# Gated products of two feed-forward sublayers as seven block products (Strassen) in a two-layer hybrid backbone

## The chip, the cores and the metric

The kernel runs on one core of a Trainium2 chip. The metric is the device time of one execution in microseconds (us). TensorE (PE) multiplies, VectorE (DVE) and ScalarE (ACT) do elementwise work, GpSimd (POOL) does little, and SyncE (SP) issues the DMAs. The kernel before took 2584.07 us, the median of three runs (2581.18 to 2584.51).

## The reference

Two streams of 256 tokens each, the latent tokens x and the context tokens ctx, of width D = 1024, go through two layers. A layer is a feed-forward sublayer, a mixer and another feed-forward sublayer; each is modulated by vectors that come from a conditioning vector (adaLN) and closed by a layer norm. In the last layer the context leaves after the first feed-forward sublayer has fed it to the mixer.

```python
def swiglu(u, w1, w3, w2):
    return (jax.nn.silu(u @ w1) * (u @ w3)) @ w2

def ffn_sublayer(h, mod, w1, w3, w2, g, b):
    u = h * (1 + mod[1]) + mod[0]
    return layer_norm(ALPHA * h + 0.5 * mod[2] * swiglu(u, w1, w3, w2), g, b)

# per layer l, with the same weights for both streams
x = ffn_sublayer(x, ada_x[0], ffn_w1[l, 0], ffn_w3[l, 0], ffn_w2[l, 0], ...)
xc = ffn_sublayer(xc, ada_c[0], ffn_w1[l, 0], ffn_w3[l, 0], ffn_w2[l, 0], ...)
# mixer of both streams, then the sublayer with index 1 (in the last layer for x alone)
```

Here w1 and w3 are 1024 x 2816 and w2 is 2816 x 1024, all in fp32. 2816 columns are FT = 22 tiles of 128.

## The kernel before, in words

Everything is kept feature-major: a tile holds 128 features in its partitions and tokens along its free axis, columns 0 to 255 (`XR`) for x and 256 to 511 (`CR`) for ctx. Three feed-forward sublayers work on 512 tokens, `ffn(0,0)`, `ffn(0,1)` and `ffn(1,0)` (layer, index); the last one, `ffn(1,1)`, on the 256 of x.

Each fp32 product is done as three products of rounded parts. `wchunk` (L186) loads a 128 x 1024 weight chunk into a buffer `raw` by an SP DMA of 512 KB, ACT writes its rounded part `whi` (L196), and DVE the remainder `wlo` (L197). The moving operand has the same two parts, made by `split_into` (L200 to L202). `mm3` (L208) then issues, for each of the 8 pieces of 128 input features, whi times high, whi times low, and wlo times high (L214, L215, L216), all into one PSUM bank.

In `ffn` the function `gated` makes the 22 tiles of silu(u @ w1) * (u @ w3): per tile two weight chunks, 2 x 8 x 3 = 48 matmuls of 512 columns, a silu on ACT (L471), a multiplication on DVE (L472) and a split into `gh` (ACT) and `gl` (DVE). The tiles are consumed in three groups, 0 to 5, 6 to 13 and 14 to 21: tiles up to one past a group are made first, then the group is multiplied by its w2 chunks, 8 chunks per group, added to the residual by DVE (L418). The last group closes the sublayer with the layer norm (`closing`).

The vectors of adaLN are made in between. `ada_job` loads pieces of w_ada (512 KB each) and DVE multiplies and adds them into accumulators `acc` (L247, L249), 32 instructions of 512 columns per job with two streams, half as many with one stream. The jobs wait in a queue; each `wchunk` lets some steps of it be issued (`tick`, with the rates RA0, RA1, RA2, in hundredths of a step), in three batches: J0 = 7 jobs during `ffn(0,0)`, J1 = 4 during `ffn(0,1)`, and the other 5 during `ffn(1,0)`.

The order on each engine is set by a scheduler: it issues what is ready, in program order, and weight work is moved ahead by 140 instructions (`PRE`). Buffers come from pools with a fixed number of slots: 4 for `raw` (NR), 5 each for the high and low weight parts (NW), 34 (NS) and 14 (NA) for 128 x 512 tiles.

Of the kernel before, what the change touches and what calls it, by code (L numbers as in the profile page):

```python
# [51 lines left out]
def hybrid_kernel(tc, x, ctx, pos, cc, wada, pcol, w1, w3, w2a, w2b, wst, wv, wg, wbr, wout, dfc, dft, idn, lnrow, out):  # L52
# [76 lines left out]

    RT = cst.tile([P, 512], F32, name="RT")  # L130
    RM = cst.tile([P, 512], F32, name="RM")
    RMh = cst.tile([P, 512], F32R, name="RMh")
    RMl = cst.tile([P, 512], F32R, name="RMl")
# [3 lines left out]
    nc.gpsimd.memset(RT, 0.0)  # L137
    nc.gpsimd.memset(RM, 0.0)
# [60 lines left out]

    def split_into(h, l, src):  # L200
        first = act(h, src, AF.Copy)  # L201
        return first, V.tensor_tensor(l, src, h.bitcast(F32), op=ALU.subtract)  # L202
# [15 lines left out]
    def proj(tiles, X, nk, T, halves):  # L218

        parts = [XR, CR] if halves and T == 512 else [slice(0, T)]  # L220
        for r in parts:
            for ps, W, *x_only in tiles:
                if r == XR or not any(x_only):
                    mm3(ps[:, r], W, X, range(nk), r)

# [126 lines left out]
    def new_operand(T):  # L352
        return [pair("op", T) for _ in range(KT)]

    def modulate(src, U, dt, l, sub, s, r):
        u = own("u", 3, 256, 256)
        act(u, src, AF.Identity, scale=modcol(l, sub, 0, s, dt), bias=modcol(l, sub, 1, s, dt))
        split_into(U[dt][0][:, r], U[dt][1][:, r], u)

# [61 lines left out]
    def closing(ys, l, sub, T, get_chunk, X, ks, nxt):  # L421
# [28 lines left out]
        U = new_operand(T)  # L450
# [5 lines left out]
    def ffn(l, i, X, ys, T, nxt):  # L456
        sub = 2 * i
        G = {}

        def gated(fts, halves=False):  # L460
# [6 lines left out]
            proj(tiles, X, KT, T, halves)  # L467
            for n, ft in enumerate(fts):
                p1, p3 = tiles[2 * n][0], tiles[2 * n + 1][0]
                sg = aslot("sg", T)  # L470
                act(sg, p1[:, 0:T], AF.Silu)  # L471
                V.tensor_tensor(sg, p3[:, 0:T], sg, op=ALU.mult)  # L472
                G[ft] = pair("g", T) if T == TX else (aslot("gh", T, F32R), slot("gl", T, F32R))
                split_into(G[ft][0], G[ft][1], sg)
# [3 lines left out]
        for ft in range(2, 7):  # L478
            gated([ft])
        for gi, grp in enumerate(GROUPS):  # L480
# [15 lines left out]
            for ft in range(grp[-1] + 2, min(grp[-1] + 10, FT)):  # L496
                gated([ft])
        return U

# [14 lines left out]
    def mixer(l, X, ys, nxt):  # L514
# [16 lines left out]
        for dt in range(KT):  # L531
            nc.sync.dma_start(out=hs[dt], in_=ys[dt][:, 0:TQ])
        gs = aslot("gs")
# [484 lines left out]
NA = 14  # L1018
NR = 4
# [3 lines left out]

TAIL = 4

J0 = 7
J1 = 4

RA0 = 135
RA1 = 75  # L1030
RA2 = 75
# [114 lines left out]
```

## Time and profile before

| | |
|---|---|
| median of three runs | 2584.07 us |
| the profiled execution | 2583.85 us |
| its span, first to last instruction | 2582.0 us |
| PE busy | 2527.9 us (98%) |
| DVE busy | 1791.0 us (69%) |
| ACT busy | 963.2 us (37%) |
| DMA, share of 16 engines | 43.8% |

Busy time counts the time in which at least one instruction of an engine was running. A matmul's listed duration is longer than the distance at which matmuls follow each other, since they are pipelined; what one costs is read from the starts of a run of them. The same holds, by a smaller amount, for DVE instructions that stand back to back.

### The profile page before, as it was taken

Reading aid. Unit: us, or ns where it says so; the run is one execution under the profiler, and the core shown is the slowest. Engines: PE = TensorE matmul, PEld = TensorE weight load, DVE = VectorE, ACT = ScalarE, POOL = GpSimd, SP = SyncE. Lnnn points to the kernel's source line nnn. Section 1 sums busy time; section 2 is a strip of 40 time slices with the busy share of each in tenths; the row PEclk is TensorE's granted clock in tenths of the full one; section 3 lists DMA queues with packets and bytes.
Section 4 is the critical chain, followed back from the end, with each engine's and each line's share of the span. In section 5 each row is a group of like instructions: output and inputs, shape, how many; then the busy total and the mean of one; then the engine's idle time right before and its main releaser. Section 6 shows DMA issues by size and latency. Waiting matters only on the chain.

```text
span 2582.0 us, 36788 instructions
## 1 busy us (share of the span) xinstructions
PE 2527.9 (98%) x14354; PEld 2143.6 (83%) x14354; DVE 1791.0 (69%) x3239; ACT 963.2 (37%) x1566; POOL 49.1 (2%) x124
## 2 busy tenths in 40 slices
PE   7999999999999999999999999999999999999998
PEld 4777779788778888888777788777788889999998
DVE  4786866978868765358656458544558888987665
ACT  4222235333342334235222225222236435455543
POOL 0000000010100000000000000000000000000000
PEclk9999999999999999999999999999999999999999
DMA  8565553213223223335445425544533334556563
GB/s 272 177 206 174 179 177 99 94 57 98 70 87 106 86 75 118 102 103 160 142 147 155 127 78 160 167 149 138 156 107 112 113 114 140 167 181 189 173 195 131
DMA packets 130542, 353.88 MB, mean 137 GB/s; under 512 B 12736, under 2 KB 28352, under 8 KB 130368
## 3 DMA queue, kind: packets, MB, share of 16 engines
q1 hardware_dynamic: 130368, 351.53, 43.8%
q8 instruction: 113, 1.85, 0.3%
q14 instruction: 61, 0.50, 0.1%
HBM read 344.11 MB, written 7.34 MB: 136 GB/s over the span
## 4 chain that ended last, share of the span: by engine, by line
PE 85%; DVE 9%; DMA 2%; ACT 1%; issue 1%; POOL 1%; SPq 0%; DVEq 0%; POOLq 0%; ACTq 0%
PE ffps L214 10%; PE ffps L216 10%; PE ffps L215 10%; PE w2ps L214 4%; PE w2ps L215 4%; PE w2ps L216 4%; PE clo L214 3%; PE br L215 3%; PE clo L215 3%; PE br L214 3%; PE clo L216 3%; PE br L216 2%; PE mg L214 2%; PE mg L216 2%; PE mg L215 2%; DVE wlo L197 2%
## 5 line engine op out<-in xcount | busy, mean ns | idle before, releaser
L196 ACT ACTIVATE whi<-raw 128x1024 fp32r<-128x1024 f32 (+1 forms) x498 | 520.5, 1047 | 1196.0 <-issue 278.6
L197 DVE TENSOR_TENSOR wlo<-raw,whi 128x1024 fp32r<-128x1024 f32 (+1 forms) x498 | 599.9, 1206 | 352.1 <-ACT whi L196 347.2
L214 PE MATMUL ffps<-opH,whi 128*128 128x512 f32 (+1 forms) x1120 | 428.4, 386 | 0.6 <-ACT opH L201 0.5
L215 PE MATMUL ffps<-opL,whi 128*128 128x512 f32 (+1 forms) x1120 | 428.8, 385 | 0.1
L216 PE MATMUL ffps<-opH,wlo 128*128 128x512 f32 (+1 forms) x1120 | 428.3, 384 | 0.4 <-DVE wlo L197 0.4
L510 DVE SCALAR_TENSOR_TENSOR cy<-cz,dww,cy 128x482 f32<-128x482 f32 (+29 forms) x480 | 289.1, 602 | 16.9 <-ACT cy L598 9.9
L249 DVE SCALAR_TENSOR_TENSOR acc<-araw,sc,acc 128x512 f32<-128x512 f32 x392 | 273.7, 746 | 30.0 <-DMA araw<-in_wada_dram 29.0
L214 PEld LDWEIGHTS ffps<-opH,whi 128*128 128x128 f32 x1120 | 209.8, 188 | 49.8 <-issue 4.6
L215 PEld LDWEIGHTS ffps<-opL,whi 128*128 128x128 f32 x1120 | 210.7, 188 | 46.0 <-issue 2.3
L216 PEld LDWEIGHTS ffps<-opH,wlo 128*128 128x128 f32 x1120 | 210.8, 189 | 45.7 <-issue 1.2
L214 PE MATMUL w2ps<-gh,whi 128*128 128x512 f32 x336 | 133.8, 398 | 0.0
L216 PE MATMUL w2ps<-gh,wlo 128*128 128x512 f32 x336 | 133.2, 397 | 0.0
L215 PE MATMUL w2ps<-gl,whi 128*128 128x512 f32 x336 | 133.0, 396 | 0.0
L472 DVE TENSOR_TENSOR sg<-ffps,sg 128x512 f32<-128x512 f32 (+1 forms) x88 | 54.7, 622 | 112.5 <-PE ffps L216 112.4
L214 PE MATMUL mg<-opH,whi 128*128 128x512 f32 (+1 forms) x384 | 130.0, 339 | 0.0
L216 PE MATMUL mg<-opH,wlo 128*128 128x512 f32 (+1 forms) x384 | 129.9, 338 | 0.0
L215 PE MATMUL mg<-opL,whi 128*128 128x512 f32 (+1 forms) x384 | 129.8, 338 | 0.0
L214 PE MATMUL qk<-opH,whi 128*128 128x512 f32 (+1 forms) x296 | 102.5, 347 | 0.0
L215 PE MATMUL qk<-opL,whi 128*128 128x512 f32 (+1 forms) x296 | 101.5, 343 | 0.0
L216 PE MATMUL qk<-opH,wlo 128*128 128x512 f32 (+1 forms) x296 | 101.1, 342 | 0.0
L214 PE MATMUL ffps<-op,whi 128*128 128x256 f32 x352 | 97.1, 280 | 3.2 <-ACT op L201 3.2
L215 PE MATMUL ffps<-op,whi 128*128 128x256 f32 x352 | 97.5, 279 | 0.0
(326 smaller groups left out, 5265.1 us busy)
## 6 DMA issues: line engine op xcount, KB each, us to landing
raw<-in_w_dram SPq DMA_DIRECT2D x176, 512.0 KB, 3.7
raw<-in_wst_dram SPq DMA_DIRECT2D x144, 512.0 KB, 3.5
araw<-in_wada_dram SPq DMA_DIRECT2D x128, 512.0 KB, 4.0
raw<-in_w2b_dram SPq DMA_DIRECT2D x64, 512.0 KB, 3.6
raw<-in_wbr_dram SPq DMA_DIRECT2D x48, 512.0 KB, 3.6
raw<-in_w2a_dram SPq DMA_DIRECT2D x32, 384.0 KB, 3.3
araw<-in_wada_dram SPq DMA_DIRECT2D x32, 256.0 KB, 5.4
raw<-in_wv_dram SPq DMA_DIRECT2D x16, 512.0 KB, 3.5
```

The lines of the kernel that those rows point to most:

```text
L196: act(hi, raw, AF.Copy)
L197: V.tensor_tensor(lo, raw, hi.bitcast(F32), op=ALU.subtract)
L214: PE.matmul(ps, wh, xh, start=first and i == 0, stop=False)
L215: PE.matmul(ps, wh, xl, start=False, stop=False)
L216: PE.matmul(ps, wl, xh, start=False, stop=last and i == n - 1)
L249: V.scalar_tensor_tensor(accs[s], w, c, accs[s], op0=ALU.mult, op1=ALU.add)
L472: V.tensor_tensor(sg, p3[:, 0:T], sg, op=ALU.mult)
L510: V.scalar_tensor_tensor(dv[:, :, a:b], sv[:, :, a + o:b + o], wcols[:, j:j + 1], dv[:, :, a:b], op0=ALU.mult, op1=ALU.add)
```

## The change

In `ffn(0,1)` and `ffn(1,0)` the tiles 4 to 21, 18 in each, are no longer made by `gated`. One such tile is seen as a 2 x 2 block product: the weights [w1 first half, w1 second half; w3 first half, w3 second half], each block 128 outputs by 512 input features, times the tokens [x first half, ctx first half; x second half, ctx second half], each block 512 features by 256 tokens. The variant of Strassen's method that is used takes seven block products in place of eight. It needs sums of weight blocks for each tile (`wquads`) and sums of token blocks once per sublayer (`Blocks.sums`).

`wquads` loads the two chunks, splits w1 (`wa`) and the second half of w3 (`wd`), makes four sums of 512 columns on DVE in the raw buffers, and splits the results (`wb`, `wc`). The low part of `wb` is made without DVE: ACT writes the rounded part with its sign changed, and a DMA issued by POOL adds the raw sum into it (`accum_op=ALU.add`). `block` multiplies one block: 4 pieces x 3 = 12 matmuls of 256 columns, 84 per tile. Four products of a tile, those with `wa` first half, `wc` first half, `wb` first half and `wd`, are added one after another into the bank `q1`, which ACT copies after the first three; those with `wb` second half and `wc` second half are added into `q3`, and the one with `wa` second half goes into `q2`. The work of one tile is interleaved with the end of the tile before (`more`).

Tiles 0 to 3 of these sublayers stay eight products, now as 256-column matmuls for each stream. Four constant tiles become scratch tiles of the mixer, zeroed by POOL there. The pools grow (NA 14 to 16, NR 4 to 5), and the adaLN jobs are dealt out anew: 9, 3 and 4 in place of 7, 4 and 5.

```diff
-    RT = cst.tile([P, 512], F32, name="RT")
-    RM = cst.tile([P, 512], F32, name="RM")
-    RMh = cst.tile([P, 512], F32R, name="RMh")
-    RMl = cst.tile([P, 512], F32R, name="RMl")
-    nc.gpsimd.memset(RT, 0.0)
-    nc.gpsimd.memset(RM, 0.0)
...
+    def wquads(src1, src3):
+        H = slice(0, 512), slice(512, 1024)
+        with tc.high_priority(offset=PRE):
+            raw = []
+            for src in (src1, src3):
+                t = wp.tile([P, 1024], F32, tag="raw", bufs=NR, name=nm("raw"))
+                nc.sync.dma_start(out=t, in_=src)
+                raw.append(t)
+            r1, r3 = raw
+            def halves(name, w=1024):
+                return [wp.tile([P, 1024], F32R, tag=t, bufs=NW, name=nm(name + t))[:, :w] for t in ("hi", "lo")]
+            a = halves("wa")
+            split_into(a[0], a[1], r1)
+            d = halves("wd", 512)
+            split_into(d[0], d[1], r3[:, H[1]])
+            add = dict(op=ALU.add)
+            V.tensor_tensor(r3[:, H[1]], r3[:, H[0]], r3[:, H[1]], **add)
+            V.tensor_tensor(r3[:, H[0]], r3[:, H[0]], r1[:, H[0]], **add)
+            V.tensor_tensor(r1[:, H[0]], r3[:, H[1]], r1[:, H[0]], **add)
+            V.tensor_tensor(r1[:, H[1]], r1[:, H[0]], r1[:, H[1]], **add)
+            b = halves("wb")
+            act(b[0], r3, AF.Copy)
+            act(b[1], b[0].bitcast(F32), AF.Copy, scale=-1.0)
+            nc.gpsimd.dma_start(out=b[1].bitcast(F32), in_=r3, accum_op=ALU.add)
+            c = halves("wc")
+            split_into(c[0], c[1], r1)
+        return (a, 0), (a, 512), (d, 0), (b, 512), (c, 0), (b, 0), (c, 512)
...
+    def block(ps, W, X, first):
+        (hi, lo), c = W
+        how = dict(skip_group_check=not first)
+        for k, (xh, xl) in enumerate(X):
+            wh, wl = (w[:, c + k * P:c + (k + 1) * P] for w in (hi, lo))
+            PE.matmul(ps, wh, xh, start=first and k == 0, stop=False, **how)
+            PE.matmul(ps, wh, xl, start=False, stop=False, **how)
+            PE.matmul(ps, wl, xh, start=False, stop=k == 3, **how)
...
     def modulate(src, U, dt, l, sub, s, r):
+        if isinstance(U, Blocks):
+            u = U.u[dt][:, r]
+            act(u, src, AF.Identity, scale=modcol(l, sub, 0, s, dt), bias=modcol(l, sub, 1, s, dt))
+            split_into(U.x[s][dt][0], U.x[s][dt][1], u)
+            return
...
+    class Blocks:
+        def __init__(self):
+            self.u = [slot("u") for _ in range(KT)]
+            self.x = [[pair("op", TX) for _ in range(KT)] for _ in range(2)]
+        def sums(self):
+            self.t = []
+            for k in range(4):
+                a, b = self.u[k], self.u[k + 4]
+                p, q = aslot("tp"), aslot("tq")
+                V.tensor_tensor(p[:, XR], a[:, XR], a[:, CR], op=ALU.subtract)
+                V.tensor_tensor(p[:, CR], b[:, CR], a[:, CR], op=ALU.subtract)
+                V.scalar_tensor_tensor(q[:, XR], p[:, XR], -1.0, b[:, CR], op0=ALU.mult, op1=ALU.subtract)
+                V.scalar_tensor_tensor(q[:, CR], q[:, XR], -1.0, b[:, XR], op0=ALU.mult, op1=ALU.subtract)
+                row = []
+                for src in (p, q):
+                    h, l = slot("tH", 512, F32R), slot("tL", 512, F32R)
+                    split_into(h, l, src)
+                    row += [(h[:, XR], l[:, XR]), (h[:, CR], l[:, CR])]
+                self.t.append(row)
+            self.u = None
+        def operands(self):
+            t1, t3, t2, t4 = ([row[n] for row in self.t] for n in range(4))
+            (x, c) = self.x
+            return x[:4], x[4:], t4, t1, t2, t3, c[4:]
...
-        U = new_operand(T)
+        U = Blocks() if T == 512 and (nxt[0], nxt[1]) in BLOCKS else new_operand(T)
...
+        def store(ft, g):
+            if T == TX:
+                G[ft] = pair("g", T)
+            else:
+                low = aslot if blocks and (ft < 4 or ft % 4 == 3) else slot
+                G[ft] = (aslot("gh", T, F32R), low("gl", T, F32R))
+            split_into(G[ft][0], G[ft][1], g)
...
+            if blocks:
+                for s, r in streams(T):
+                    for ps, W in tiles:
+                        mm3(ps[:, r], W, X.x[s], range(KT), XR)
+            else:
+                proj(tiles, X, KT, T, halves)
...
+        def start_blocks(ft):
+            f = dict(ft=ft, W=wquads(w1[l, i, ft], w3[l, i, ft]))
+            f["r1"], f["r3"] = bank(mmp, "q1")[:, XR], bank(mmp, "q3")[:, XR]
+            f["c"], f["v"] = aslot("cc"), aslot("cv", 256)
+            Q[:] = X.operands()
+            block(f["r1"], f["W"][0], Q[0], True)
+            act(f["c"][:, XR], f["r1"], AF.Copy)
+            block(f["r3"], f["W"][3], Q[3], True)
+            return f
+        def middle_blocks(f):
+            block(f["r1"], f["W"][4], Q[4], False)
+            act(f["c"][:, CR], f["r1"], AF.Copy)
+            r2 = bank(atp, "q2")[:, XR]
+            block(r2, f["W"][1], Q[1], True)
+            c = f["c"][:, XR]
+            V.tensor_tensor(c, r2, c, op=ALU.add)
+            act(c, c, AF.Silu)
+        def third_blocks(f):
+            block(f["r1"], f["W"][5], Q[5], False)
+            act(f["v"], f["r1"], AF.Copy)
+        def x_blocks(f):
+            block(f["r1"], f["W"][2], Q[2], False)
+            c = f["c"][:, XR]
+            V.scalar_tensor_tensor(c, f["r1"], -1.0, c, op0=ALU.mult, op1=ALU.mult)
+            V.tensor_tensor(f["v"], f["r3"], f["v"], op=ALU.add)
+        def ctx_blocks(f):
+            block(f["r3"], f["W"][6], Q[6], False)
+            c = f["c"][:, CR]
+            V.tensor_tensor(c, f["r3"], c, op=ALU.add)
+            act(c, c, AF.Silu)
+            V.scalar_tensor_tensor(c, f["v"], -1.0, c, op0=ALU.mult, op1=ALU.mult)
+            store(f["ft"], f["c"])
+        Q = []
+        open_ = []
+        def more(fts):
+            if not blocks:
...
+            for ft in fts:
+                f = start_blocks(ft)
+                if open_:
+                    x_blocks(open_[0])
+                middle_blocks(f)
+                if open_:
+                    ctx_blocks(open_.pop())
+                third_blocks(f)
+                open_.append(f)
+            if ft == FT - 1:
+                x_blocks(open_[0])
+                ctx_blocks(open_.pop())
...
         gated([0, 1], not ready)
         run_later()
-        for ft in range(2, 7):
-            gated([ft])
+        if blocks:
+            X.sums()
+            for ft in (2, 3):
+                gated([ft])
+            more(range(4, 7))
+        else:
+            more(range(2, 7))
...
+        RT, RM, RMh, RMl = aslot("RT"), aslot("RM"), aslot("RMh", 512, F32R), aslot("RMl", 512, F32R)
+        nc.gpsimd.memset(RT, 0.0)
+        nc.gpsimd.memset(RM, 0.0)
...
-NA = 14
-NR = 4
+NA = 16
+NR = 5
+BLOCKS = ((0, 2), (1, 0))
-J0 = 7
-J1 = 4
+J0 = 9
+J1 = 3
```

First place: ACT during one gated tile in the middle of `ffn(0,1)`, before the change (names end in a buffer's number).

```order
L196 ACTIVATE whi_10868<-raw_10866 128x1024
L257 ACTIVATE adar_10702<-adaps_10693 128x128
L201 ACTIVATE gh_10689<-sg_10686 128x512
L196 ACTIVATE whi_10875<-raw_10873 128x1024
L471 ACTIVATE sg_10770<-ffps_10714 128x512
```

The same place now: wb, wc, wa and wd are the weight parts above; cv and cc receive what is copied out of the banks.

```order
L220 ACTIVATE wbhi_11274<-raw_11260 128x1024
L586 ACTIVATE cv_11152<-q_1778_11149 128x256
L221 ACTIVATE wblo_11275<-wbhi_11274 128x1024
L571 ACTIVATE cc_11285<-q_1796_11283 128x256
L229 ACTIVATE wchi_11279<-raw_11258 128x1024
L229 ACTIVATE wahi_11396<-raw_11392 128x1024
L229 ACTIVATE wdhi_11400<-raw_11394 128x512
L582 ACTIVATE cc_11285<-cc_11285 128x256
L577 ACTIVATE cc_11285<-q_1796_11283 128x256
L599 ACTIVATE cc_11151<-cc_11151 128x256
L229 ACTIVATE gh_11369<-cc_11151 128x512
```

A tile had four ACT instructions (beside adaLN's `adar`), two of them on weights; it now has eleven, five of them on weights, and the first two on `wb` have a copy out of a bank between them.

Second place: PE at the same point, before the change, where one chunk ends and the next begins.

```order
L214 MATMUL ffps_10872<-opH_9505,whi_10868 128x512
L215 MATMUL ffps_10872<-opL_9506,whi_10868 128x512
L216 MATMUL ffps_10872<-opH_9505,wlo_10869 128x512
L214 MATMUL ffps_10879<-opH_9491,whi_10875 128x512
L215 MATMUL ffps_10879<-opL_9492,whi_10875 128x512
L216 MATMUL ffps_10879<-opH_9491,wlo_10876 128x512
```

And now, where the low part of `wb` is read for the first time by a tile (`q_1815` is its bank q3, `q_1814` its bank q1).

```order
L262 MATMUL q_1814_11417<-tH_10071,wclo_11414 128x256
L260 MATMUL q_1814_11417<-tH_10085,wchi_11413 128x256
L261 MATMUL q_1814_11417<-tL_10086,wchi_11413 128x256
L262 MATMUL q_1814_11417<-tH_10085,wclo_11414 128x256
L262 MATMUL q_1815_11418<-tH_10039,wblo_11409 128x256
L260 MATMUL q_1815_11418<-tH_10053,wbhi_11408 128x256
L261 MATMUL q_1815_11418<-tL_10054,wbhi_11408 128x256
L262 MATMUL q_1815_11418<-tH_10053,wblo_11409 128x256
```

The matmuls are half as wide, the product with `wb` second half was begun 36 matmuls earlier and taken up again here, and everything behind its first `wblo` row waits for the DMA that fills `wblo`.

## Rows read from the trace of the kernel before

**Rows 1.** The page: busy time of the engines, granted clock by slices, and the chain.

```profile
PE 2527.9 (98%) x14354; PEld 2143.6 (83%) x14354; DVE 1791.0 (69%) x3239; ACT 963.2 (37%) x1566; POOL 49.1 (2%) x124
PEclk9999999999999999999999999999999999999999
PE 85%; DVE 9%; DMA 2%; ACT 1%; issue 1%; POOL 1%; SPq 0%; DVEq 0%; POOLq 0%; ACTq 0%
```

**Rows 2.** Windows, busy us by engine, granted clock, DMA share, GB/s: `ffn(0,0)`, `ffn(0,1)`.

```profile
60.00:400.00 340.00, 338.82 (x1639) 266.29 (x1638) 259.03 (x415) 95.14 (x128) 0.00 (x0) 1.00 0.58 179
1312.00:1400.00 88.00, 88.00 (x404) 70.02 (x403) 51.91 (x76) 22.52 (x29) 0.00 (x0) 1.00 0.48 144
```

**Rows 3.** Timeline of PE, 512 columns: first and last of 43 matmuls in a row.

```profile
1310.14 0.40 PE L215 MATMUL ffps<-opL,whi 128*128 128x512 f32 x1
...
1319.94 0.40 PE L215 MATMUL ffps<-opL,whi 128*128 128x512 f32 x1
```

**Rows 4.** Timeline of PE, 256 columns: first and last of 61, then of 37.

```profile
2450.14 0.28 PE L215 MATMUL ffps<-op,whi 128*128 128x256 f32 x1
...
2456.94 0.28 PE L215 MATMUL ffps<-op,whi 128*128 128x256 f32 x1
```

```profile
1525.67 0.28 PE L214 MATMUL clo<-gh,whi 128*128 128x256 f32 x1
...
1529.91 0.28 PE L214 MATMUL clo<-gh,whi 128*128 128x256 f32 x1
```

**Rows 5.** DVE by line and shape: busy us, mean ns of one, idle before.

```profile
L197 DVE TENSOR_TENSOR wlo<-raw,whi 128x1024 fp32r<-128x1024 f32 x466 | 569.4, 1223 | 334.4 <-ACT whi L196 329.5
L315 DVE TENSOR_TENSOR acc<-acc,mrg 128x256 f32<-128x256 f32 x51 | 21.5, 421 | 0.7
```

**Rows 6.** Timeline of DVE, 150 to 200 us, instructions back to back.

```profile
153.68 1.23 DVE L197 TENSOR_TENSOR wlo<-raw,whi 128x1024 fp32r<-128x1024 f32 x1
154.82 0.87 DVE L418 SCALAR_TENSOR_TENSOR y<-w2ps,ada,y 128x256 f32<-128x256 f32 x2
155.60 2.07 DVE L249 SCALAR_TENSOR_TENSOR acc<-araw,sc,acc 128x512 f32<-128x512 f32 x3
157.65 1.23 DVE L197 TENSOR_TENSOR wlo<-raw,whi 128x1024 fp32r<-128x1024 f32 x1
...
192.19 0.69 DVE L472 TENSOR_TENSOR sg<-ffps,sg 128x512 f32<-128x512 f32 x1
192.79 0.74 DVE L249 SCALAR_TENSOR_TENSOR acc<-araw,sc,acc 128x512 f32<-128x512 f32 x1
```

**Rows 7.** One window, columns as in Rows 2: DVE's fullest stretch of `ffn(0,0)`.

```profile
150.00:200.00 50.00, 50.00 (x241) 39.10 (x240) 43.08 (x70) 15.19 (x19) 0.00 (x0) 1.00 0.69 218
```

**Rows 8.** ACT by line and shape, columns as in Rows 5.

```profile
L196 ACT ACTIVATE whi<-raw 128x1024 fp32r<-128x1024 f32 x466 | 493.4, 1061 | 1099.2 <-issue 254.2 <-PE ffps L215 135.2 <-DMA raw<-in_w_dram 133.4
L201 ACT ACTIVATE gh<-sg 128x512 fp32r<-128x512 f32 x66 | 41.5, 629 | 35.8 <-DVE sg L472 35.0
L471 ACT ACTIVATE sg<-ffps 128x256 f32<-128x256 f32 x22 | 7.9, 365 | 0.0
```

**Rows 9.** DMA issues: count, KB each, median us from issue to landing.

```profile
raw<-in_w_dram SPq DMA_DIRECT2D x176, 512.0 KB, 3.7
cs<-cy SPq DMA_DIRECT2D x8, 256.0 KB, 2.2
cn<-cs SPq DMA_DIRECT2D x8, 256.0 KB, 5.6
op<-mid SPq DMA_DIRECT2D x8, 1.0 KB, 1.7
```

More of the change, by code (lines that the diff above doesn't have):

```diff
@@ L198, in wchunk @@
         return hi, lo
+    def wquads(src1, src3):
+        tick()
+        H = slice(0, 512), slice(512, 1024)
[24 more added lines that the diff above has]
+        return (a, 0), (a, 512), (d, 0), (b, 512), (c, 0), (b, 0), (c, 512)
     def split_into(h, l, src):
@@ L458, in ffn @@
         G = {}
+        blocks = isinstance(X, Blocks)
+        def store(ft, g):
[5 more added lines that the diff above has]
+            split_into(G[ft][0], G[ft][1], g)
         def gated(fts, halves=False):
@@ L466, in gated @@
                 ready.pop(ft, None)
-            proj(tiles, X, KT, T, halves)
+            if blocks:
[4 more added lines that the diff above has]
+                proj(tiles, X, KT, T, halves)
             for n, ft in enumerate(fts):
@@ L472, in gated @@
                 V.tensor_tensor(sg, p3[:, 0:T], sg, op=ALU.mult)
-                G[ft] = pair("g", T) if T == TX else (aslot("gh", T, F32R), slot("gl", T, F32R))
-                split_into(G[ft][0], G[ft][1], sg)
+                store(ft, sg)
+        def start_blocks(ft):
[7 more added lines that the diff above has]
+            return f
@@ new lines, in ctx_blocks @@
+        def ctx_blocks(f):
[11 more added lines that the diff above has]
+                    gated([ft])
+                return
+            for ft in fts:
+                f = start_blocks(ft)
[9 more added lines that the diff above has]
+                ctx_blocks(open_.pop())
@@ L476, in ffn @@
         gated([0, 1], not ready)
         run_later()
-        for ft in range(2, 7):
-            gated([ft])
+        if blocks:
+            X.sums()
+            for ft in (2, 3):
+                gated([ft])
+            more(range(4, 7))
+        else:
+            more(range(2, 7))
         for gi, grp in enumerate(GROUPS):
@@ L495, in ffn @@
                 del G[ft]
-            for ft in range(grp[-1] + 2, min(grp[-1] + 10, FT)):
-                gated([ft])
+            more(range(grp[-1] + 2, min(grp[-1] + 10, FT)))
         return U
@@ L1017 @@
 NS = 34
-NA = 14
-NR = 4
+NA = 16
+NR = 5
 NW = 5
 PRE = 140
+BLOCKS = ((0, 2), (1, 0))
 TAIL = 4
-J0 = 7
-J1 = 4
-RA0 = 135
-RA1 = 75
-RA2 = 75
+J0 = 9
+J1 = 3
+RA0 = 165
+RA1 = 80
+RA2 = 100
 RC0 = 240
```

## The prediction

> **What bounds the kernel now.** I read the page first: PE is busy for 2527.9 of 2582.0 us at a granted clock that stays in the top tenth, and the chain of waits goes through PE for 85% [rows 1]. Then the windows by stage: in the middle of `ffn(0,1)` PE is busy for 88.00 of 88 us, DVE for 51.91 and ACT for 22.52, and in `ffn(0,0)` PE for 338.82 of 340 [rows 2]. So in the feed-forward sublayers nothing but the number and distance of the matmuls sets the time, and DVE has about 40% to spare, ACT 75%. Last I read the timeline, because a matmul's listed length (0.40 us) overlaps the next. The 43 starts from 1310.14 to 1319.94 are 42 distances, 0.2333 us each at 512 columns [rows 3]. At 256 columns the distance is 0.1133 in one stretch and 0.1178 in another [rows 4]; the granted clock of the windows is 1.00, the 2.4 GHz level. Half the columns therefore cost half the time, although each matmul still loads its own weights.
>
> **Matmuls.** A gated tile was 48 x 0.2333 = 11.20 us. It becomes 84 x 0.1155 (the middle of the two distances) = 9.70, between 9.52 and 9.90. That saves 1.50 per tile, and 36 tiles give 54 us (47 to 60). Tiles 2 and 3 of the two sublayers, as 256-column matmuls, gain less than 1 us.
>
> **DVE.** A tile now has 13 DVE instructions. Their price is the distance at which they follow each other when queued: 1.14 us for a 1024 split, 0.60 for 512 columns, 0.39 for the three-operand form on 256 [rows 6], and 0.34 for the plain form on 256 (0.42 [rows 5] less the same 0.08 of overlap). Two 1024 splits, one 512 split, four sums and `gl` are 2.28 + 6 x 0.60 = 5.9; three plain and two three-operand instructions on 256 add 1.8: 7.7 us, where it was 3.5. In the order of the changed kernel 15 adaLN instructions stand between the `gl` of tile 7 and that of tile 13 of `ffn(0,1)`; at 0.68 [rows 6] they and six tiles are 56.4 us, beside 58.2 us of matmuls. So DVE is 97% full there. Before, 43.08 of 50 us with PE full throughout [rows 7] is the fullest I found. I take 3 us for waits that DVE's order passes on to PE, between nothing and the third rival below.
>
> **ACT.** The 1024 roundings of `wa`, `wb` and `wc` and the sign-changed copy are four at 1.06, two at 0.63 (`wd` and `gh`) and five short ones on 256 columns at 0.37 [rows 8]: 7.4 us of 9.7. It is hidden by PE as long as nothing waits for one of them in particular.
>
> **The refill of wb.** Here something does. The buffers of `wb` have one copy each in the order: ACT can overwrite them only when the last block product that reads the old ones (`wb` first half, into q1) has ended, and PE needs the new low part a fixed number of matmuls later. Counted in the order, 30 tiles follow another block tile directly; the first `wblo` matmul comes 47 to 50 matmuls after that end in 14 of them, 55 in one and 58 to 63 in 15, thus 48 x 0.1155 = 5.5 us or 61 x 0.1155 = 7.0 us. In this time must happen: a copy out of the bank (0.37), the rounding (1.06), mostly another copy (0.37), the sign-changed copy (1.06), together 2.8 us [rows 8], and then the DMA of POOL. No row shows a DMA issued by POOL, nor one that adds. From below: 1 KB between buffers of the core takes 1.7 and 256 KB out of them 2.2 [rows 9], so 512 KB, read once, 1.7 + 1.0 = 2.7. From above: 5.6, the slowest transfer here with nothing to compute (256 KB, `cn`) [rows 9]. The nearest row is the weight load of the same size, 3.7 us; since the destination must be read too, another 0.7 of the 1.0 that 512 KB cost, I take 4.4. Then a short interval is late by 2.8 + 4.4 - 5.5 = 1.7 and a long one by 0.2, and 14 x 1.7 + 15 x 0.2 + 1 = 28, near 27 us with unrounded lengths. At 2.7 us it is 0, at 5.6 it is 62. Behind the waiting matmul stand the rest of that product, the next copy and the first half of `wb`, so the whole of PE waits, and DVE's `q` instructions after it.
>
> The Trainium skill ("DMA: Bandwidth & Descriptors", Anatomy of one DMA) gives a POOL-issued DMA about 2.0 us plus its bytes over 436e3 per us, an estimate of 3.2 us for 512 KB; no run so far shows it. By it the short intervals would be late by 0.5, and the time would be that of the first rival. Its rules for kernel authors on the same page say that an accumulating DMA reads its destination and writes it later, which speaks for more than one pass over the bytes and against that figure.
>
> **What costs little.** The token sums are 16 DVE instructions on 256 and 8 splits on 512, 5.9 + 4.8 = 11 us per sublayer, and 5 us of ACT; the 45 us of PE in tiles 0 to 3 hide them, and without that cover it would be 11 us each. I take 2 in all. `ffn(0,0)` gets two more adaLN jobs: 64 x 0.68 = 44 us of DVE, which makes 303 of 340 us where it was 259 [rows 2]: 89%, a little over the fullest stretch so far; I take 2. The other sublayers lose one job each, which helps them. The memsets fall on POOL, busy 49.1 us of the whole [rows 1], and I give them nothing. The number of loads is the same; raw buffers are held longer, by the DMA that reads them, but there are five.
>
> **Sum.** -54 + 27 + 3 + 2 + 2 = -20 on the profiled execution's 2583.85, which stands 0.2 below the median of the runs: 2564 us.
>
> **Rivals.**
> First, the refill is hidden: the accumulating DMA takes no longer than 3.2 us, half a microsecond over the lower bound. For it speaks the 2.2 us of a 256 KB transfer [rows 9], against it that this one has two operands to read. 14 x 0.5 leaves about 7 us of waits, and -54 + 7 + 4 gives 2541.
> Second, slower: the accumulating DMA takes as long as the slowest row, 5.6. Loads share the engines with it (DMA share 0.48 [rows 2]), and it has two operands to read and one to write. The waits are 14 x 2.9 + 15 x 1.4 + 1 = 62, and -54 + 62 + 7 gives 2599. It decides from about 5.1 us on, where waits and saving cancel.
> Third, DVE becomes the bound. It stands in order, and in each tile it waits for the product with `wd`, then for the rounding of `wc` that overwrites `wd` (1.06), then for a silu and for `gh` (0.63). With 7.7 us of work, 1.7 of adaLN (15 x 0.68 over six tiles) and 1.7 of such waits a tile takes 11.1, 36 tiles save 4 us, and the small costs above take them back: 2584, no change. Against it speaks that a split, a sum or an accumulation stands between most of these pairs in the order.
>
> **How the numbers follow.** A difference under 0.2%, about 5 us, can't be told from no change. I give the forecast 0.42 (its own range 2550 to 2577), the first rival 0.22, the second 0.23, the third 0.13. Faster is 0.41 + 0.22 + 0.02 = 0.65; the same is 0.01 + 0.02 of the second + 0.07 of the third = 0.10; slower is the rest, 0.25. The range reaches from the first rival's end with the smaller matmul distance, 2534, to a little beyond the second, 2602.
>
> **What would show it.** In the profile after, 256-column matmuls of the blocks at 0.113 to 0.118 us would confirm the saving, 0.133 would undo it. The DMA issues will list the accumulating DMA's time: 4.4 by my sum, up to 3.2 or from 5.1 by the rivals. PE's waits in the two sublayers should be some 30 us, most of them at the first `wblo` row of the tiles with the short interval, released by that DMA. If DVE is busy over 95% there and PE waits for its splits instead, the third rival holds. PE busy of nearly 100% in these windows would mean the first. In `ffn(0,0)` the 340 us should stay within 5.

## The result: slower, and the profile after

The changed kernel takes 2656.7 us (median of four runs, 2654.6 to 2659.9) where the kernel before takes 2583.8: a ratio of 1.0286, 95% interval 1.0273 to 1.0299. The prediction was 2564 us with a range of 2534 to 2602. It is wrong in direction and by 93 us.

The page of the changed kernel, its lines on the engines, on the product with the low part of `wb`, and on the software queue and the new transfer (columns as in [rows 1], [rows 5] and [rows 9]):

```profile
PE 2526.0 (95%) x15842; PEld 2209.2 (83%) x15842; DVE 1960.8 (74%) x3611; ACT 1108.7 (42%) x1834; POOL 80.4 (3%) x162
...
q0 software_dynamic: 5184, 18.88, 4.0%
...
L262 PE MATMUL q<-tH,wblo 128*128 128x256 f32 x288 | 92.1, 320 | 74.3 <-DMA wblo<-raw 74.3
...
wblo<-raw POOLq DMA_DIRECT2D x36, 512.0 KB, 4.8
```

PE is busy as long as before [rows 1], though it has less to do, and has 74.3 us of idle time ahead of the matmuls of one line, all released by one transfer. The windows, as [rows 2], say where: `ffn(0,0)`, then the block tiles of `ffn(0,1)` and of `ffn(1,0)`.

```profile
60.00:400.00 340.00, 336.77 (x1670) 260.77 (x1670) 290.32 (x464) 90.70 (x119) 1.05 (x2) 1.00 0.63 198
1296.00:1396.00 100.00, 86.35 (x678) 80.80 (x677) 74.34 (x123) 53.61 (x84) 6.95 (x8) 0.98 0.56 148
1708.00:1817.00 109.00, 91.26 (x681) 86.18 (x680) 68.56 (x115) 54.30 (x87) 6.88 (x8) 0.91 0.55 152
```

Where PE was busy for 88 of 88 us before, it is for 86 of 100 and 91 of 109, at a granted clock of 0.98 and 0.91. DVE has 26 and 37% to spare there. The first matmul of the two sublayers and the last of the second, from PE's timeline (start, us), before and after:

```profile
1167.11 0.28 PE L214 MATMUL ffps<-opH,whi 128*128 128x256 f32 x1
...
1551.63 0.28 PE L214 MATMUL ffps<-opH,whi 128*128 128x256 f32 x1
...
1936.15 0.28 PE L216 MATMUL clo<-gh,wlo 128*128 128x256 f32 x1
```

```profile
1171.96 0.28 PE L242 MATMUL ffps<-op,whi 128*128 128x256 f32 x1
...
1583.04 0.28 PE L242 MATMUL ffps<-op,whi 128*128 128x256 f32 x1
...
2014.46 0.28 PE L244 MATMUL clo<-gh,wlo 128*128 128x256 f32 x1
```

`ffn(0,1)` takes 411.1 us (384.5 before) and `ffn(1,0)` 431.4 (384.5): together 73.5 us more, nearly all of the 76.0 by which the two traced executions differ (the medians differ by 72.9). From all start-to-start distances of PE in the two sublayers:

| part | us |
|---|---|
| 1704 more matmuls of 256 columns at 0.1155, 960 fewer of 512 at 0.2333 | -27 each, -54 |
| waits at the first `wblo` matmul: 74.3 of idle time and 6 for its own weight load, then exposed | +80 |
| about 230 matmuls at the 1.2 GHz level, in 14 runs | +23 |
| pieces of 0.05 to 0.3 us, mostly at matmuls that carry a wait and the one behind them | +25 |

The sum is 74; the last class is the least certain, 23 to 30 by where its bounds are drawn. So the saving came as predicted, and three things took it back with 74 us on top.

**A usual refill.** ACT, POOL and PE of one tile, from their timelines; the last matmul with the old `wb` had started at 1362.37.

```profile
1362.62 1.06 ACT L220 ACTIVATE wbhi<-raw 128x1024 fp32r<-128x1024 f32 x1 [1.18 <-issue]
1363.59 0.37 ACT L586 ACTIVATE cv<-q 128x256 f32<-128x256 f32 x1
1363.85 1.05 ACT L221 ACTIVATE wblo<-wbhi 128x1024 fp32r<-128x1024 f32 x1
...
1365.20 0.87 POOL L222 DMA_DIRECT2D wblo<-raw  x1 [10.71 <-ACT cc L571]
...
1369.99 0.39 PE L262 MATMUL q<-tH,wblo 128*128 128x256 f32 x1 [1.07 <-DMA wblo<-raw]
```

That is 0.25 + 2.3 on ACT, 0.3 to POOL, 4.8 for the transfer: 7.6 us; the shortest of all took 7.5. The interval here is the short one, 48 matmuls. In the next tile, with a long interval (59 matmuls), the last matmul with the old `wb` started at 1373.74, and the refill takes 9.4 us. The buffer is free, but what is to be rounded is not there yet. VectorE makes it with two sums (L214, L215) behind the split of `wd`, and that split starts here only 0.2 us behind PE's last matmul with a `wc` (1372.15):

```profile
1372.36 0.63 ACT L229 ACTIVATE wdhi<-raw 128x512 fp32r<-128x512 f32 x1
1373.02 0.69 DVE L230 TENSOR_TENSOR wdlo<-raw,wdhi 128x512 fp32r<-128x512 f32 x1
...
1373.96 0.69 DVE L214 TENSOR_TENSOR raw<-raw 128x512 f32<-128x512 f32 x1
...
1374.96 0.69 DVE L215 TENSOR_TENSOR raw<-raw,raw 128x512 f32<-128x512 f32 x1
...
1375.74 1.06 ACT L220 ACTIVATE wbhi<-raw 128x1024 fp32r<-128x1024 f32 x1 [0.53 <-DVE raw L215]
```

The sum is late in all 16 tiles with an interval of 55 to 63 matmuls: it ends 0.8 to 2.3 us after the start of the last matmul with the old `wb`, and in 14 of them the rounding begins 0.1 us behind it. In the 14 tiles with 47 to 50 the sum ended 1.7 to 7.6 us before that matmul.

**A long refill.** Here a weight load of SP is issued 0.62 us behind the transfer. The transfer takes 7.6 us instead of 4.8, PE waits 3.95 us, and the 22 matmuls behind follow at 0.21 us instead of 0.1155:

```profile
1880.24 0.86 POOL L222 DMA_DIRECT2D wblo<-raw  x1 [12.72 <-DVE cc L592]
...
1880.86 1.98 SPq L202 DMA_DIRECT2D raw<-in_w_dram  x2
...
1887.88 0.58 PE L262 MATMUL q<-tH,wblo 128*128 128x256 f32 x1 [3.95 <-DMA wblo<-raw]
1888.26 0.42 PE L260 MATMUL q<-tH,wbhi 128*128 128x256 f32 x1
1888.48 0.41 PE L261 MATMUL q<-tL,wbhi 128*128 128x256 f32 x1
1888.69 0.41 PE L262 MATMUL q<-tH,wblo 128*128 128x256 f32 x1
```

I listed all 36 transfers with the loads issued near them. Of 14 that took 5.9 to 7.6 us, 13 had a load issued between 0.7 us before and 1.5 us after them; of the 22 that took 4.5 to 5.3, none (the nearest load was 1.06 us before). The 22 cost 25.6 us of waiting (0.6 to 1.6 each), the 14 cost 48.7 (2.7 to 5.3 each). Of 14 pauses of PE over 1.8 us (2.8 to 5.5 from start to start, less a matmul), 13 were followed within 1.1 us by 10 to 27 matmuls at half rate; no shorter pause was.

### The profile page after: what moved, and what is told of

It is laid out like the page before. It is cut to its first block, busy times and chain, and to the rows that moved or that the text cites. A ratio compares the mean times of both kernels' runs of the same rounds, so it can differ in the third digit from the quotient of the medians.

```text
span 2658.0 us, 40621 instructions
## 1 busy us (share of the span) xinstructions
PE 2526.0 (95%) x15842; PEld 2209.2 (83%) x15842; DVE 1960.8 (74%) x3611; ACT 1108.7 (42%) x1834; POOL 80.4 (3%) x162
## 5 line engine op out<-in xcount | busy, mean ns | idle before, releaser
L189 ACT ACTIVATE whi<-raw 128x1024 fp32r<-128x1024 f32 (+1 forms) x426 | 444.2, 1045 | 837.2 <-issue 166.6
L190 DVE TENSOR_TENSOR wlo<-raw,whi 128x1024 fp32r<-128x1024 f32 (+1 forms) x426 | 511.7, 1203 | 253.3 <-ACT whi L189 250.2
L242 PE MATMUL ffps<-op,whi 128*128 128x256 f32 x608 | 165.2, 281 | 3.8 <-ACT op L229 3.8
L243 PE MATMUL ffps<-op,whi 128*128 128x256 f32 x608 | 167.8, 280 | 0.0
L244 PE MATMUL ffps<-op,wlo 128*128 128x256 f32 x608 | 167.2, 279 | 0.0
L262 PE MATMUL q<-tH,wblo 128*128 128x256 f32 x288 | 92.1, 320 | 74.3 <-DMA wblo<-raw 74.3
L242 PE MATMUL ffps<-opH,whi 128*128 128x512 f32 x352 | 141.5, 404 | 0.9 <-ACT opH L229 0.9
L243 PE MATMUL ffps<-opL,whi 128*128 128x512 f32 x352 | 140.9, 401 | 0.0
L244 PE MATMUL ffps<-opH,wlo 128*128 128x512 f32 x352 | 140.4, 401 | 0.4 <-DVE wlo L190 0.4
L242 PEld LDWEIGHTS ffps<-op,whi 128*128 128x128 f32 x608 | 113.1, 190 | 4.7 <-ACT op L229 4.2
L243 PEld LDWEIGHTS ffps<-op,whi 128*128 128x128 f32 x608 | 114.7, 189 | 0.3 <-DVE op L230 0.2
L244 PEld LDWEIGHTS ffps<-op,wlo 128*128 128x128 f32 x608 | 114.7, 189 | 0.0
```

The lines of the kernel that those rows point to most:

```text
L189: act(hi, raw, AF.Copy)
L190: V.tensor_tensor(lo, raw, hi.bitcast(F32), op=ALU.subtract)
L242: PE.matmul(ps, wh, xh, start=first and i == 0, stop=False)
L243: PE.matmul(ps, wh, xl, start=False, stop=False)
L244: PE.matmul(ps, wl, xh, start=False, stop=last and i == n - 1)
L262: PE.matmul(ps, wl, xh, start=False, stop=k == 3, **how)
```

## The experiments

The theory (A) was that PE stands until the refill of `wb` has come through the transfer, and that this standing brings the clock down. The rivals: the block products themselves lower the clock (B), VectorE is the bound (C), the transfer slows the other engines (D), the other edits cost the time (E).

| run | ratio to before, 95% interval | us | the two sublayers, us | waits for the low part of `wb` | half rate, us |
|---|---|---|---|---|---|
| before | 1 | 2583.8 | 384.5 + 384.5 | - | 0 |
| changed | 1.0286 (1.0273 to 1.0299) | 2656.7 | 411.1 + 431.4 | 74.3 | 23 |
| e1 subtraction on DVE | 0.9938 (0.9921 to 0.9954) | 2567.0 | 375.7 + 371.1 | 3.5 | 2 |
| e2 no transfer | 0.9912 (0.9896 to 0.9929) | 2559.7 | 371.5 + 369.4 | 1.4 | 2 |
| e3 own slot for `wd` | 1.0797 (1.0781 to 1.0814) | 2787.9 | 474.1 + 475.4 | 13.8 | 56 |
| e4 no block products | 0.9993 (0.9984 to 1.0002) | 2579.5 | 382.2 + 381.5 | - | 0 |
| e5 low part last | 1.0309 (1.0275 to 1.0344) | 2663.0 | 418.6 + 423.9 | 76.3 | 20 |
| e6 four raw buffers | 1.0334 (1.0313 to 1.0356) | 2670.2 | 411.0 + 426.1 | 67.0 | 20 |
| e7 two half transfers | 1.0229 (1.0206 to 1.0253) | 2643.5 | 405.9 + 417.3 | 55.0 | 18 |
| e8 DVE, two `wd` slots | 0.9973 (0.9958 to 0.9988) | 2578.2 | 373.6 + 368.9 | 1.3 | 5 |
| e9 weight loads after | 1.0223 (1.0205 to 1.0242) | 2643.5 | 409.9 + 412.5 | 54.4 | 17 |
| e10 all loads after | 1.0494 (1.0473 to 1.0515) | 2712.6 | 436.2 + 451.3 | 35.9 | 24 |
| e11 subtraction on POOL | 1.0193 (1.0174 to 1.0211) | 2635.5 | 409.4 + 406.1 | 49.2 | 10 |
| e12 e1, prepared earlier | 0.9967 (0.9955 to 0.9979) | 2576.0 | 379.9 + 371.4 | 2.4 | 3 |
| e13 e1, no copies of the bank | 0.9929 (0.9913 to 0.9946) | 2564.9 | 372.2 + 375.4 | 0.7 | 3 |
| e14 e8, old adaLN spread | 1.0020 (1.0008 to 1.0032) | 2586.8 | 385.5 + 388.0 | 2.0 | 0 |

**e1, the subtraction on VectorE**

```diff
-            act(b[0], r3, AF.Copy)
-            act(b[1], b[0].bitcast(F32), AF.Copy, scale=-1.0)
-            nc.gpsimd.dma_start(out=b[1].bitcast(F32), in_=r3, accum_op=ALU.add)
+            split_into(b[0], b[1], r3)
```

> One part of the change replaced: the low part of the combined weights is made by a VectorE subtraction (about 1.2 us, as for the other weights) instead of a copy on ScalarE and an accumulating transfer (4.8 us from issue to landing). The slots stay as they are. Theory A (the refill of one slot pair, longest because of the transfer, makes TensorE wait 74 us, and these waits bring the granted clock down, another 45 us): the waits fall under 15 us, the granted clock returns to 1.00 in the block stretches, time 2540 to 2565. Theory B (the lower clock belongs to the 256-column block products themselves): waits fall, but some 45 us of half-clock matmuls stay, 2580 to 2610. Theory C (VectorE is close to the bound, which is why the subtraction was given to a transfer): TensorE waits for VectorE instead, 40 us or more, time 2590 or above.

Its page, and the longest waits of PE in the two sublayers (us in total, times, longest):

```profile
PE 2490.4 (97%) x15842; PEld 2179.0 (85%) x15842; DVE 1997.2 (78%) x3647; ACT 1074.8 (42%) x1798; POOL 49.1 (2%) x126
```

```profile
PE q L260 <- DVE wblo L228: 3.5, 4, 2.0
PE q L258 <- ACT wbhi L227: 2.7, 5, 0.9
PE q L258 <- ACT wchi L227: 2.5, 4, 0.9
```

The waits for `wblo` fall to 3.5 us and the half rate to 2, with the same block products: B falls, and C too, since DVE does 36 us more and PE waits for it only six times in the two sublayers, 4.9 us in all. The time is 2 us beyond the expected end. This version beats both kernels, the one before by 0.6%.

**e2, the transfer left out**

```diff
-            nc.gpsimd.dma_start(out=b[1].bitcast(F32), in_=r3, accum_op=ALU.add)
```

> Leaves out the accumulating transfer: the low part of the combined weights is then only the negated high part, so that part of the weights' low bits is wrong; every other instruction is there. Theory A: the refill after the last use of the slot is two ScalarE copies (2.1 us), waits under 10 us, clock 1.00, time 2535 to 2560. Theory B (clock falls with the block products): 2580 to 2600. A rival for the transfer's price (D: its reads and writes slow other engines' access rather than that it lands late): the other engines' mean durations, the VectorE split of 1024 columns above all, fall by over 5% against the changed kernel; A expects them the same within 2%.

2559.7 is within A. In the two sublayers the 1024-column splits of `wa` and `wc` on DVE, most of which run while the transfer is under way, take 1221 ns each with it and 1224 without, so D falls: the transfer costs by landing late.

**e3, a slot pair of its own for `wd`**

```diff
-            d = halves("wd", 512)
+            d = [wp.tile([P, 512], F32R, tag="d" + t, bufs=1, name=nm("wd" + t)) for t in ("hi", "lo")]
-NR = 5
+NR = 4
```

> The transfer stays, the wait for the slot goes: the 512-column weights get a slot pair of their own (half as wide), so that the combined weights no longer take the slots of the tile before and are made ahead; raw buffers 4 instead of 5 to pay for it. Theory A: the transfer still takes about 4.8 us from issue to landing, TensorE's waits for it fall from 74 us to under 10, clock 1.00, time 2535 to 2560. Theory D or B: the transfer is still there and so are the lower clock or the slower engines, 2580 or above.

It failed: 2788. The waits for the transfer did fall, to 13.8 us, but others took their place:

```profile
PE q L260 <- ACT wchi L229: 57.8, 34, 1.7
PE q L260 <- ACT wbhi L220: 45.7, 34, 1.9
PE q L262 <- DMA wblo<-raw: 13.8, 17, 3.9
```

ACT's timeline of one tile says why:

```profile
1504.82 0.64 ACT L229 ACTIVATE wdhi<-raw 128x512 fp32r<-128x512 f32 x1 [0.86 <-PE q L261]
...
1507.93 1.06 ACT L220 ACTIVATE wbhi<-raw 128x1024 fp32r<-128x1024 f32 x1 [0.24 <-DVE raw L215]
...
1520.69 0.63 ACT L229 ACTIVATE wdhi<-raw 128x512 fp32r<-128x512 f32 x1 [0.91 <-PE q L261]
```

With one slot `wd` can be rounded only when the product with the old one has ended, and the split of `wd`, the sums, `wb` and `wc` stand behind it in order: the whole preparation now starts from PE in each tile, every 15.9 us. I had moved the single slot from one operand to an earlier one of the same chain. It is the chain of the long intervals above, now in every tile. It says nothing against A, and shows that a slot's price depends on what stands behind it.

**e4, all but the block products**

```diff
-BLOCKS = ((0, 2), (1, 0))
+BLOCKS = ()
```

> Everything of the change but the block products: no sublayer takes them, but the buffer numbers, the place of four constants and the spread of the adaLN jobs are as in the changed kernel. Theory A: within 0.4% of before (2578 to 2595), the first feed-forward sublayer some 6 us longer, the two sublayers in question 384 us each as before. Theory E (the spread of the jobs and the buffers carry a good part of the loss): 2600 or above.

The other edits cost nothing in sum, so E falls. `ffn(0,0)` ends 9.7 us later than before (433.8 against 424.1), and the two sublayers are 2.3 and 3.0 us shorter: the adaLN jobs moved.

**e5, more matmuls for the refill**

```diff
+            for k, x in enumerate(X):
+                for n in range(2):
+                    PE.matmul(ps, hi[:, c + k * P:c + (k + 1) * P], x[n], start=k + n == 0, stop=False, **how)
+            for k, x in enumerate(X):
+                PE.matmul(ps, lo[:, c + k * P:c + (k + 1) * P], x[0], start=False, stop=k == 3, **how)
```

> The first product that reads the combined weights does its eight matmuls with the high part first and the four with the low part last. In the order this puts the first matmul on the low part 58.5 matmuls on average after the last use of the slot, where it was 53.4: 0.6 us more for the refill of each of 36 tiles. Theory A (TensorE stands until the transfer lands): waits for it fall from 74 to 80 us by some 20, to 55 to 62, time 2630 to 2645. Theory F (the transfer takes 6 to 7.6 us only where a weight load is issued close to it, those long waits alone drop the clock): besides, waits of over 2.5 us stay followed by 10 to 27 half-clock matmuls and shorter ones by none. If TensorE itself were the bound: no change, 2657.

It failed in the size: 76.3 us of waits, as without. The order gave the refill 0.6 us more, and on ACT the rounding of `wb` then began 1.62 us after the end of the old product on average, where it was 1.13: in 20 of the 30 tiles that follow another block tile it began within 0.11 us of the end of VectorE's second sum, where 14 did. So the start moved with the room, and each wait stayed. That the scheduler's plan has the transfer shorter than it is would explain it; no run shows the plan's figure. The half-clock rows agree with F in the main: ten of the 12 pauses over 2.5 us were followed by a granted clock of 0.50, but so were two of the four between 1.8 and 2.5.

**e6, four raw buffers**: `NR = 5` becomes `NR = 4`.

> Four raw buffers instead of five, so that a weight load can't be issued before a raw buffer of the running tile is free, which is after the accumulating transfer has started. Theory F (a load issued within about 1.5 us of that transfer makes it 6 to 7.6 us long instead of 4.8; these 13 of 36 cause the long waits and the clock losses): at most 5 transfers over 5.5 us, waits from 80 to 40 to 55 us, half-clock time from 23 to under 8, time 2595 to 2625. Rival G (long transfers come by chance or from the second sublayer's own traffic): as many long ones, time 2645 to 2670. Rival H (loads now come too late): TensorE waits for the splits of wa, wc or wd, over 2670.

It failed: 11 transfers over 5.5 us are left, 8 of them with a load close by, waits 67.0. The loads were not kept away from the transfers, so the run could not tell F from G. It also reaches `ffn(0,1)` at 1187.6 us instead of 1172.0 (e14).

**e7, the transfer in two halves**

```diff
+            for h in reversed(H):
+                nc.gpsimd.dma_start(out=b[1].bitcast(F32)[:, h], in_=r3[:, h], accum_op=ALU.add)
```

> The accumulating transfer as two of 256 KB, the half that is read first sent first; the order leaves 47 matmuls on average for it (53.4 before), 0.75 us less. If the transfer's time goes with its bytes (half of 4.8 us less some fixed part: 3.0 to 3.6 for the first half), waits fall to 35 to 60 us and the time to 2605 to 2640. If it is a fixed time for each transfer, or two share the engines so that the first half lands at 4.5 or later, waits grow to 90 or more, time 2665 to 2690.

The first half lands after 3.3 us in 18 of 36 tiles, the waits fall by 19 us though the order leaves 0.75 us less: bytes count. 13 first halves still took 4.3 us or more, and all of these had a load issued within 0.8 us before to 0.6 us after; of the 23 shorter ones none had one as near. The time is 3.5 us beyond the range.

**e8, the subtraction and two slot pairs for `wd`**: e1, with `bufs=2` in the line of e3, `NR = 4`, `NA = 14`.

> The VectorE subtraction instead of the transfer, and two slot pairs of half width for the 512-column weights (paid for with four raw buffers and 14 slots of the gated products). Without the transfer raw buffers are free sooner. Theory A: the remaining waits of the subtraction alone (about 20 us in the two sublayers) fall to under 12, time 2552 to 2565. If VectorE's order is what is left: 2560 to 2575, with TensorE waiting for VectorE's splits. If the chain of the splits (raw, wd, sums, wb) becomes late as with the single slot pair: over 2600.

The two sublayers are 4.3 us shorter than in e1, but `ffn(0,1)` starts at 1190.0 us instead of 1171.3, so it is slower than e1. PE's idle time in the two sublayers did not fall as expected: 16.3 us, where e1 has 16.4.

**e9, weight loads kept behind the transfer**

```diff
+                load = nc.sync.dma_start(out=t, in_=src)
+                if len(sent) > 1:
+                    after(load, sent[-2])
```

> The weight loads of a block tile wait until the accumulating transfer of the tile two before has landed; the transfer itself, the slots and the buffers are as in the changed kernel. In the changed kernel 13 of 36 transfers had a load issued within 0.7 us before to 1.5 us after them and took 5.9 to 7.6 us (the 22 without one 4.5 to 5.2, one 7.0); eight of these loads were weights, five adaLN. Theory F (such a load lengthens the transfer; the long wait that follows lowers the clock): 4 to 8 transfers over 5.5 us are left, those beside adaLN loads, waits for the transfer 80 to 60 us or less, half-clock time 23 to about 10, time 2620 to 2640. Rival G (long transfers have another cause): 12 to 15 long ones, 2650 or above. Rival H (loads too late): TensorE waits for splits, 2660 or above.

PE's longest wait in the two sublayers:

```profile
PE q L266 <- DMA wblo<-raw: 54.4, 34, 4.6
```

Seven transfers over 5.5 us are left, five with a load close by, and 29 take 4.5 to 5.5. F holds: with the loads moved and nothing else, the waits fall by 20 us and the half rate by 6, to 17 where about 10 was expected. The time, 2643, is 3 us beyond the range. Over the changed kernel, e5, e6 and e9, a load issued 1.0 us before to 1.6 us after stood beside 41 of the 48 transfers over 5.5 us, and beside one of the 96 others.

**e10, the adaLN loads too**: `after(load, sent[-1])` in `ada_job`.

> As the run before, and the adaLN loads too wait for the last transfer that was issued ahead of them. Theory F: at most 3 transfers over 5.5 us, waits 40 to 52 us (36 of 1.1 to 1.4), half-clock time under 6 since no wait is over 2.5 us, time 2600 to 2620. Rival G: unchanged, 2650 or above. Rival H: loads stand in one queue, so weights behind a held adaLN load come late, 2640 or above with TensorE waiting for splits or loads.

The waits for the transfer fell to 35.9 us, below F's range, and the time rose, as H has it:

```profile
PE q L266 <- DMA wblo<-raw: 35.9, 28, 4.8
PE q L264 <- ACT wchi L233: 23.5, 14, 1.9
PE q L264 <- ACT cv L592: 11.3, 17, 2.2
```

Five transfers of 5.6 to 6.2 us stay, four with no load issued within 5 us; what lengthens those I did not find.

**e11, the subtraction on GpSimd**

```diff
+            nc.gpsimd.tensor_tensor(b[1], r3, b[0].bitcast(F32), op=ALU.subtract)
```

> The low part of the combined weights by a subtraction on GpSimd, which is nearly idle, instead of copy and transfer. No trace here shows such an instruction on GpSimd. If it takes no longer than on VectorE (1.2 us): like the run without the transfer, 2555 to 2570. If it takes some 2 to 3 us: waits of 10 to 40 us, 2570 to 2610. If it also slows VectorE's instructions while it runs: VectorE's mean durations of 1024-column splits over 1.25 us, and more.

The page's rows of PE and POOL, then POOL and DVE of one tile on the timeline:

```profile
L261 PE MATMUL q<-tH,wblo 128*128 128x256 f32 x288 | 85.3, 296 | 49.2 <-POOL wblo L221 49.2
...
L221 POOL TENSOR_TENSOR wblo<-raw,wbhi 128x1024 fp32r<-128x1024 f32 x36 | 90.9, 2524 | 596.4 <-ACT wbhi L220 596.4
```

```profile
1717.87 2.36 POOL L221 TENSOR_TENSOR wblo<-raw,wbhi 128x1024 fp32r<-128x1024 f32 x1 [11.54 <-ACT wbhi L220]
...
1717.16 0.68 DVE L216 TENSOR_TENSOR raw<-raw,raw 128x512 f32<-128x512 f32 x1
1717.88 2.90 DVE L217 TENSOR_TENSOR raw<-raw 128x512 f32<-128x512 f32 x1
```

2.5 us on average, and the DVE sum that runs beside it takes 2.90 us here and 2.7 to 2.9 in 25 of the 36 tiles, where it is 0.69 in the changed kernel. The waits come to 49 us and the time is beyond the expected 2610.

**e12, e1 prepared earlier**: `PRE = 180`.

> The VectorE subtraction, with weight preparation given a higher priority in the planner (180 places ahead instead of 140). The subtraction alone waits some 20 us in the two sublayers, a third of it at the first block tile of a stretch, where the splits come late. If earlier preparation mends these: 2555 to 2565. If what is left are the hand-overs between banks and copies: within 3 us of 2567.

9 us slower than e1, and the waits are much the same (2.4 us at `wblo`; 17.1 us of PE's idle time of all kinds, 16.4 in e1). Neither answer holds.

**e13, no product waits for a copy of its bank**

```diff
-            act(f["c"][:, XR], f["r1"], AF.Copy)
+            act(f["c"][:, XR], Q[0][0][0].bitcast(F32), AF.Copy)
```

and so for the two other copies.

> The VectorE subtraction, and the three copies per tile out of the bank that collects four products now read a matrix of the tokens instead, so that the gated values are made from wrong numbers; the same instructions run, but no product waits for a copy of its bank. If the hand-overs come from this bank: the 20 us or so of small delays in the two sublayers fall under 8, time 2548 to 2558. If they come from the waits for weights: delays as before, 2560 to 2570.

Small delays at matmuls that carry a wait, with the exposed weight load behind them, fall from 20 us in e1 to 14, and the time does not change, since the waits for the rounding of `wc` rise from 2.5 to 9.0 us. So about a third comes from the bank; for the rest the weights' own waits are left, which I did not test one by one.

**e14, e8 with the adaLN jobs as before**: `J0 = 7`, `J1 = 4`, rates 135, 75, 75.

> The subtraction with two slot pairs of half width, four raw buffers and 14 slots as in e8, but with the spread of the adaLN jobs as before the change. If the four raw buffers are too few only for the new spread: the second feed-forward sublayer starts at 1167 to 1173 us instead of 1190, time 2555 to 2568. If four buffers are too few in any case: 2575 or above.

`ffn(0,1)` starts at 1165.4 us, so four buffers are too few only for the new spread. But the sublayers become 31 us longer than in e8, with PE waiting for adaLN:

```profile
PE adaps L290 <- DVE acc L285: 15.9, 6, 5.8
PE clo L240 <- ACT whi L189: 7.1, 2, 6.7
```

The change needed to take adaLN work out of these sublayers, and five raw buffers to do it.

## Why the prediction was wrong

**The saving.** Right as a price: 256-column matmuls follow at 0.115 us on average at the full clock, and -54 is what the count gives.

**The step that failed is the refill of `wb`**: "14 x 1.7 + 15 x 0.2 + 1 = 28, near 27 us", with bounds of 0 and 62. It measured 74 us of waiting. That PE stands at the first `wblo` matmul until the transfer has landed was right; the size was not. By the prediction's own classes of tiles:

| tiles | predicted, us | measured, us | with a usual transfer | with one of 5.9 us or more |
|---|---|---|---|---|
| 14 with 47 to 50 matmuls | 24 | 25.0 | 9 of 1.2 | 5 of 2.8 |
| 16 with 55 to 63 | 4 | 30.3 | 11 of 1.1 | 5 of 3.6 |
| 6 that open a stretch | 0 | 18.9 | 2 of 1.2 | 4 of 4.1 |

- The short intervals came out right by luck. A usual wait is 1.2 and not 1.7: the transfer takes 4.8 where I took 4.4, but the matmuls and what stands between them last 6.5 us in the tile shown (1362.37 to 1369.99, less the wait of 1.07) where I had 5.5. Long transfers made up the rest.
- "A long one by 0.2": I summed the way from the free buffer and left out the way to what is rounded into it. VectorE's second sum ends up to 2.3 us after the last use, so the long intervals give no more room than the short ones. This is read from the trace; no run moved the sums.
- The six first tiles of a stretch had no term, without a reason. In four of them the rounding of `wb` is released by a product with w2 (`PE w2ps` in the trace), in a fifth by VectorE's second sum.
- "5.6, the slowest transfer here" as upper end: 14 transfers took 5.9 to 7.6, and 13 had a load close by (e9 moved loads and the waits fell). Their waits are 48.7 us; at 1.2 each they would be 17, so their length cost about 32. I named shared engines in the second rival, but as a reason for one fixed duration.

The order of PE leaves little room: 24 of the 84 matmuls read `wb`, so at most 62 lie between the last use and the first low matmul, 7.2 us (68 or 7.9 us with the low part last, as in e5). The shortest refill is 7.5, and those of the long intervals with a usual transfer take 8.1 to 9.6. Other orders were not run.

**No term stood for what a wait costs beyond itself.** The half rate (+23) and the small delays (+25) were put at nothing. e1 has the small delays without the transfer: against e4 its sublayers save 17 us, not 54, with about 20 lost there and 18 in waits of under 2.1 us.

**The small terms.** DVE's order (+3), token sums (+2): the products wait for DVE 0.6 us in all. What DVE's order cost went through the refill, as above. `ffn(0,0)`: DVE is busy 290 of 340, I had 303; the sublayer ends at 430.5 us, 6.4 later than before, where I took 2 and said within 5.

**The rivals.** The second, slower, was the right one, with its deciding point at 5.1 us of transfer. The mean over all 36 is above it, but its price of 2599 rested on the same formula. The first (hidden) and the third (DVE) are refuted by the page and e1. The Trainium skill ("DMA: Bandwidth & Descriptors", Anatomy of one DMA) led to an estimate of 3.2 us; the measured 4.8 decides. The Trainium skill's rule (same page, Rules for kernel authors) that an accumulating DMA reads the destination and writes it later spoke for the longer time; no run here has the same transfer without the adding, so that this is the reason is not shown.

## What to carry to other kernels

Look for an operand whose slot has one copy, and sum two ways to its next use: from its last use (the engine's queue in its real order, hand-overs, the transfer beside other transfers), and from whatever makes the data that goes into it. Do it for the first tile of a stretch too. Compare the later end with the interval that the order gives. If it doesn't fit, try to take the transfer out before reordering: a 1.2 us subtraction on a VectorE with a quarter to spare was worth 90 us here. Price a wait of PE at more than its length.

## What the runs showed that I had not expected

- A transfer of 512 KB between buffers that adds took 4.5 to 5.5 us in 95 of the 102 cases with no load issued close to it (median 4.8 in the changed kernel), and 5.5 to 9.1 us in 41 of the 42 with one (changed kernel, e5, e6 and e9).
- In the changed kernel 13 of the 14 pauses of PE of 2.8 us or more, and no shorter one, were followed by 10 to 27 matmuls at the 1.2 GHz level; the trace has 13 stretches there with a granted clock of 0.50. That does not carry over to the other runs: in e3 33 of 35 pauses of 1.8 to 2.8 us were followed by such a stretch too, and in e1 and e2 two pauses of about 1 us close together were. The window around the long refill shown above, and 2.5 us of it:

```profile
1880.00:1900.00 20.00, 15.96 (x114) 15.01 (x113) 11.97 (x21) 9.30 (x15) 1.72 (x2) 0.83 0.53 139
1888.30:1890.80 2.50, 2.50 (x13) 2.50 (x13) 0.00 (x0) 0.00 (x0) 0.00 (x0) 0.50 0.70 202
```

- A matmul that waited costs another 0.1 us. Its weight load starts with it, where the next one's is 0.11 us ahead: 0.22 us to the next start at 1369.99, where 0.1155 is usual.

```profile
1369.99 0.19 PEld L262 LDWEIGHTS q<-tH,wblo 128*128 128x128 f32 x1 [1.28 <-DMA wblo<-raw]
1369.99 0.39 PE L262 MATMUL q<-tH,wblo 128*128 128x256 f32 x1 [1.07 <-DMA wblo<-raw]
1370.10 0.19 PEld L260 LDWEIGHTS q<-tH,wbhi 128*128 128x128 f32 x1
1370.21 0.28 PE L260 MATMUL q<-tH,wbhi 128*128 128x256 f32 x1
```

- A 128 x 1024 subtraction on GpSimd took 2.5 us where VectorE takes 1.2, and a VectorE sum of 0.69 us took 2.7 to 2.9 beside it in 25 of 36 tiles (e11).
